# A mixture-of-experts stage on one core: the gated product is turned behind the down products and behind the branch, and the expert counts are read before the first gate and up products

## The chip, the core and the metric

The kernel runs on one core of one Trainium2 chip. A core has five engines that run side by side: TensorE (PE, matrix products; its weight loads are shown as PEld), VectorE (DVE), ScalarE (ACT), GpSimd (POOL) and SyncE (SP, which here only issues transfers). Each engine takes its instructions in order, and waits for the others through semaphores. Products land in PSUM, everything else lies in SBUF, and weights come from HBM by DMA. The metric is the device time of one execution in microseconds.

## The reference, cut to what matters

Two blocks of a model of 256 tokens and width 1024 are computed in float32. The part that is changed is the mixture-of-experts layer of the first block:

```python
def moe_ffn(h, router_w, router_b, w_gate, w_up, w_down):
    t = h.reshape(bsz * seq, d)
    logits = t @ router_w + router_b
    top_v, top_i = lax.top_k(logits, 2)
    gates = jax.nn.softmax(top_v, axis=-1)
    combine = jnp.sum(jax.nn.one_hot(top_i, 8) * gates[..., None], axis=1)
    out = jnp.zeros((bsz * seq, d))
    for e in range(8):
        y_e = (silu(t @ w_gate[e]) * (t @ w_up[e])) @ w_down[e]
        out = out + combine[:, e:e + 1] * y_e
    return out
```

There are 8 experts, each token goes to 2 of them, and an expert's hidden width is 3584. An expert's weights are 3 matrices of 1024 x 3584 in float32, 42 MB (42 x 1,048,576 bytes), and the whole layer reads 336 MB.

## The kernel before

**Stages.** The program runs ten stages one after the other: two mixers, a dense feed-forward stage, the mixture-of-experts stage (`moe`), and then the stages of the second block. Only `moe` is changed. In it the tokens of an expert are gathered into up to 96 slots (`xe`), 32 slots to a group; groups 0 and 1 (64 slots) are called `main`, group 2 is `rest`.

**Blocks.** An expert's hidden width is worked off in 7 blocks of 512, so the loop of `moe` passes 56 blocks, i = 0 to 55, expert by expert, and one more pass at its end. A block has three steps:

- `gate_up(i, gs)`: on PE, products of the gathered tokens with the block's gate and up weights (line 1098), then on ACT the silu of the gate half (line 1102) and on DVE its product with the up half (line 1103). The result is the tile `gs`.
- `turn_g(i, gs)`: on PE, transposes of `gs` (line 1110; two for `main`, one for `rest`), and an ACT copy to the tile `gT` (line 1112).
- `down(i, gs)`: on PE, products of `gT` with the block's down weights into an accumulator of the expert (line 1126).

`down` runs one block late (`LAG = 1`): pass i does `gate_up(i)`, then `down(i - 1)`, then `turn_g(i)`. The steps for `rest` stand in a block `tc.If(counts[e] > 64)` (line 1191), so they run only for experts that got more than 64 tokens. On the chip each engine takes that branch by itself; an engine that skips the body still brings its semaphores to the values that the body would have left. In the first pass of an expert the `rest` part of `down` belongs to the expert before and has an If of its own. Another If (line 1180), in pass 15, skips a large body that handles experts with more than 96 tokens; these inputs do not need it.

**Order.** The instructions are laid out by a scheduler before the kernel runs. It gives each engine one fixed order, picks by the order of the source and by when it thinks that operands will be there, and treats an If as one piece. So the order on PE in the trace is not always that of the source: `turn_g`'s transposes stand in some blocks ahead of `down`'s products and in others behind them, and half of `down` can stand behind the If. `tc.issue_after(ins)` forces what is traced inside it to be issued behind `ins` on the engine of `ins`, without a wait.

**Weights.** The layer's 336 MB come as 336 units of 1 MB, in the order of use: 4 units of gate and up for block i, then 2 of down for block i - 1. SP issues one transfer for each unit (line 217). A unit needs a buffer; in this stage there are 16 of them, 15 later on. At the end of pass i, `W.give` hands back the buffers of the block's 4 units and of the 2 of `down`, and the next 6 units are issued into them when PE has passed the last reader, the If included.

**Counts.** `R.counts` holds the tokens of each expert. `values_load_multi_w_load_instructions` (line 1171) loads it into registers of all engines, for the branches to compare. In the source it stands behind the first `gate_up`.

Of the kernel before, what the change touches and what calls it, by code (L numbers as in the profile page):

```python
# [20 lines left out]
T = 256  # L21
NE = 8
# [250 lines left out]
def model(ctx, tc, A, out, stages=STAGES):  # L273
    nc = tc.nc
# [94 lines left out]
    def bank(tag="mm"):  # L369
        p = mm if tag == "mm" else acc  # L370
        return p.tile([128, 512], F32, tag=tag, name=tag)
# [673 lines left out]
    def moe(R, nout, pool):  # L1045


        nb = F1 // 512
# [13 lines left out]
        def gather(p):  # L1062
            S[p] = pool.tile([128, 2, 2, SLOTS], F32R, tag="S", name="S", bufs=2)
            for t in range(2):
                for e in range(2):
                    nc.vector.tensor_scalar(S[p][:, t, e], iota[:, :SLOTS], R.pos[:, t, 2 * p + e:2 * p + e + 1],
                                            R.sel[:, t, 2 * p + e:2 * p + e + 1], ALU.is_equal, ALU.mult)
            xe[p] = pool.tile([128, 8, 2, SLOTS], F32, tag="xe", name="xe", bufs=2)
            w = 2 * SLOTS
            for j in range(4):  # L1070
                ps = bank()
                for i in range(2):
                    k = 2 * j + i
                    o = ps[:, i * w:(i + 1) * w]
                    for t in range(2):
                        s = S[p][:, t].rearrange("p e s -> p (e s)")
                        nc.tensor.matmul(o, R.h[t][:, k * 128:(k + 1) * 128], s, start=t == 0, stop=False)
                        nc.tensor.matmul(o, R.l[t][:, k * 128:(k + 1) * 128], s, start=False, stop=t == 1)
                v = ps[:, :2 * w].rearrange("p (k e s) -> p k e s", k=2, e=2)
                if j % 2:  # L1080
                    nc.vector.tensor_copy(xe[p][:, 2 * j:2 * j + 2], v)
                else:
                    nc.scalar.activation(xe[p][:, 2 * j:2 * j + 2], v, AF.Copy)

        def strips(gs):

            return [(g, c) for g in gs for c in range(4 // len(gs))]

        def gate_up(i, gs):
            e, b = seq[i]  # L1090
            if ("gu", i) not in held:
                held["gu", i] = [W.hold(((("moe", e), "gu", b), j)) for j in range(4)]
            units = held["gu", i]
            n = 256 * len(gs)
            ps = bank()
            for k in range(8):
                for j, (g, c) in enumerate(strips(gs)):
                    nc.tensor.matmul(ps[32 * j:32 * j + 32, :n], xe[e // 2][:, k, e % 2, 32 * g:32 * g + 32],  # L1098
                                     units[k // 2][0](k % 2, c * n, n), start=k == 0, stop=k == 7)
            s = prod[i, gs] = tp.tile([128, 512], F32, tag="g32", name="gs", bufs=4)[:, :n // 2].rearrange("p (q c) -> p q c", c=128)  # L1100
            v = ps[:, :n].rearrange("p (q s c) -> p q s c", s=2, c=128)
            nc.scalar.activation(s, v[:, :, 0], AF.Silu)  # L1102
            nc.vector.tensor_tensor(s, v[:, :, 1], s, op=ALU.mult)  # L1103

        def turn_g(i, gs):

            s, n = prod.pop((i, gs)), len(gs)
            ps = bank()
            for q in range(n):
                nc.tensor.transpose(ps[:, q * 128:(q + 1) * 128], s[:, q], ident)  # L1110
            a = gT[i, gs] = pool.tile([128, n, 128], F32, tag=f"gT{gs[0]}", name="gT", bufs=LAG + 1)
            nc.scalar.activation(a, ps[:, :n * 128].rearrange("p (q c) -> p q c", q=n), AF.Copy)

        def down(i, gs):
            e, b = seq[i]
            if ("d", i) not in held:
                held["d", i] = [W.hold(((("moe", e), "d", b), j)) for j in range(2)]
            units = held["d", i]
            n, w = len(gs), 256 * len(gs)
            if b == 0:  # L1120
                y[e, gs] = bank("acc")
            a, o = gT.pop((i, gs)), y[e, gs]
            for k in range(4):
                for j, (g, c) in enumerate(strips(gs)):
                    at = (k // n + (g - gs[0]) * 2) * 32
                    nc.tensor.matmul(o[32 * j:32 * j + 32, :w], a[:, k % n, at:at + 32], units[k // 2][0](k % 2, c * w, w),  # L1126
                                     start=b == 0 and k == 0, stop=b == nb - 1 and k == 3)
            if b == nb - 1:
                if e not in yf:
                    yf[e] = pool.tile([SLOTS, D], F32, tag="yf", name="yf", bufs=1)  # L1130
                    nc.gpsimd.memset(yf[e][64:SLOTS], 0.0)
                for j, (g, c) in enumerate(strips(gs)):
                    r, v = yf[e][32 * g:32 * g + 32, c * w:(c + 1) * w], o[32 * j:32 * j + 32, :w]
                    if j % 2:
                        nc.vector.tensor_copy(r, v)
                    else:
                        nc.scalar.activation(r, v, AF.Copy)

        def back(e):
            yh, yl = (a.rearrange("p c t -> p (c t)")[:SLOTS] for a in xt())  # L1140
            nc.scalar.activation(yh, yf[e], AF.Copy)
            nc.vector.tensor_tensor(yl, yf[e], yh.bitcast(F32), op=ALU.subtract)
            ST = pool.tile([SLOTS, 2, 128], F32R, tag="ST", name="ST", bufs=1)
            ps = bank()
            for t in range(2):
                nc.tensor.transpose(ps[:SLOTS, t * 128:(t + 1) * 128], S[e // 2][:, t, e % 2, :].bitcast(F32), ident)
            nc.scalar.activation(ST, ps[:SLOTS, :256].rearrange("p (t s) -> p t s", t=2), AF.Copy)

            def scatter(ts=range(2)):
                for t in ts:  # L1150
                    for q in range(2):
                        ps = bank()
                        for n, a in enumerate((yh, yl)):
                            nc.tensor.matmul(ps, ST[:, t, :], a[:, q * 512:(q + 1) * 512], start=n == 0, stop=n == 1)
                        xs = X[t][:, q * 512:(q + 1) * 512]
                        nc.vector.scalar_tensor_tensor(xs, ps, R.comb[:, t, e:e + 1], xs, ALU.mult, ALU.add)
            todo.append(scatter)


        main, rest = (0, 1), (2,)  # L1160
        n = len(seq)
        gather(0)
        for i in range(n + LAG):
            j = i - LAG
            now, late = [], []
            if i < n:
                e, b = seq[i]
                gate_up(i, main)
                now.append(lambda: gate_up(i, rest))
            if i == 0:  # L1170
                _, counts = nc.values_load_multi_w_load_instructions(R.counts[0:1, :NE + 1], min_val=0, max_val=T,
                                                                     skip_runtime_bounds_check_because="the values are only compared")
            if i == 2:
                R.gates()
            if i == n - 2:
                nout.post = post_of(A["final_g"])
            while todo:
                todo.popleft()()
            if i == 2 * nb + 1:
                with tc.If(counts[NE] > SLOTS):  # L1180
                    for base in range(SLOTS, T, 128):
                        second(R, base)
            if j >= 0:
                down(j, main)
                (now if i < n and seq[j][0] == e else late).append(lambda: down(j, rest))
            if i < n:
                turn_g(i, main)
                now.append(lambda: turn_g(i, rest))
            for at, fs in ((j, late), (i, now)):
                if fs:  # L1190
                    with tc.If(counts[seq[at][0]] > 64):  # L1191
                        for f in fs:
                            f()
            W.give(held.pop(("gu", i), []) + held.pop(("d", j), []))
            if j >= 0 and seq[j][1] == nb - 1:
                back(seq[j][0])
            if i < n and e % 2 == 1 and b == nb - 3 and e < NE - 1:
                gather(e // 2 + 1)
        last = todo.popleft()
# [149 lines left out]
```

## Time and profile before

| what | value |
|---|---|
| three runs | 2337.69, 2341.61, 2342.85 us; median 2341.61 |
| the profiled execution's own time | 2337.93 us |
| its span, first to last instruction | 2336.1 us (1.8 us lie around it) |
| PE busy over the span | 2227.8 us, 95% |
| DVE, ACT, POOL busy | 40%, 34%, 7% |
| mean granted TensorE clock | 0.989 |
| HBM read | 595 MB, 255 GB/s over the span |

The trace is that of one execution. Times in it are microseconds from the first instruction; the `moe` stage's products run from 434.3 to 1298.9. An engine's busy share says little here, since matmuls overlap one another; what counts is the time from the start of one step to the start of the next, and the idle time that a row shows in brackets.

### The profile page before, as it was taken

The numbers are of one execution on the slowest core, as the hardware profiler recorded it, in microseconds if no ns is written. First come the engines' busy times: TensorE is split into PE (matmuls) and PEld (weight loads), VectorE is DVE, ScalarE is ACT, GpSimd is POOL, SyncE is SP. The second block draws the span as 40 slices with busy tenths as digits, with TensorE's granted clock in tenths as the row PEclk, the third lists the DMA queues.
The fourth block names the chain that finished last, engine by engine and source line by source line (L and its number), as shares of the span: only waits on it lengthen the run. The fifth ranks groups of instructions, "written<-read, shape, count | busy, mean of one in ns | idle before, by whom it ended". The sixth has DMA issues, their size and how long they took to land. (4 is left out here: it accounts for less than half of the span.)

```text
span 2336.1 us, 36130 instructions
## 1 busy us (share of the span) xinstructions
PE 2227.8 (95%) x15276; PEld 1487.4 (64%) x15276; DVE 926.2 (40%) x1246; ACT 793.3 (34%) x1243; POOL 172.5 (7%) x258
## 2 busy tenths in 40 slices
PE   8999999899989999999998899989999999989998
PEld 7888888434433333333432588877888888877887
DVE  5655565201010101010010554577544644686544
ACT  5544444201010101011010444466444534575443
POOL 3000013000000000000000200061000100050000
PEclk9999999899999999999999999999999999999999
DMA  7655555799979999999999655441555555423552
GB/s 272 226 186 192 180 202 184 288 419 419 420 296 370 382 419 419 401 397 419 420 420 397 250 182 186 152 163 46 198 186 190 183 180 184 154 108 117 182 186 85
DMA packets 89436, 599.09 MB, mean 256 GB/s; under 512 B 12092, under 2 KB 14558, under 8 KB 18460
## 3 DMA queue, kind: packets, MB, share of 16 engines
q1 hardware_dynamic: 88956, 595.81, 65.8%
q8 instruction: 144, 2.36, 0.4%
q10 hardware_dynamic: 288, 0.52, 0.1%
q14 instruction: 48, 0.39, 0.0%
HBM read 595.25 MB, written 1.05 MB: 255 GB/s over the span
## 5 line engine op out<-in xcount | busy, mean ns | idle before, releaser
L238 DVE TENSOR_TENSOR wl<-raw,wh 128x1024 fp32r<-128x1024 f32 (+2 forms) x456 | 540.3, 1215 | 429.0 <-ACT wh L237 428.6
L237 ACT ACTIVATE wh<-raw 128x1024 fp32r<-128x1024 f32 (+2 forms) x456 | 454.6, 1036 | 482.6 <-PE mm L398 302.2
L1098 PE MATMUL mm<-raw,xe 128*32 128x512 f32 (+1 forms) x5376 | 504.2, 525 | 2.7 <-DVEq L1191 1.8
L395 PE MATMUL mm<-wh,xhl 128*128 128x512 f32 (+3 forms) x1280 | 473.5, 372 | 3.1 <-ACT xhl L414 3.1
L396 PE MATMUL mm<-wl,xhl 128*128 128x512 f32 (+3 forms) x1280 | 471.9, 371 | 0.5 <-DVE wl L238 0.5
L398 PE MATMUL mm<-wh,xhl 128*128 128x512 f32 (+3 forms) x1280 | 394.4, 371 | 0.6 <-DVE xhl L415 0.6
L1098 PEld LDWEIGHTS mm<-raw,xe 128*32 128x32 f32 x5376 | 181.3, 111 | 296.3 <-issue 251.0
L1103 DVE TENSOR_TENSOR gs<-mm,gs 128x256 f32<-128x256 f32 (+1 forms) x84 | 31.9, 380 | 688.4 <-ACT gs L1102 590.9
L395 PEld LDWEIGHTS mm<-wh,xhl 128*128 128x128 f32 x1280 | 241.8, 189 | 43.9 <-ACT xhl L414 3.5
L1126 PE MATMUL acc<-raw,gT 128*32 128x512 f32 (+1 forms) x2688 | 266.0, 526 | 3.5 <-PEq L1191 2.7
L396 PEld LDWEIGHTS mm<-wl,xhl 128*128 128x128 f32 x1280 | 241.7, 189 | 41.3 <-DVE wl L238 1.3
L398 PEld LDWEIGHTS mm<-wh,xhl 128*128 128x128 f32 x1280 | 236.8, 189 | 41.5 <-DVE xhl L415 1.7
L1102 ACT ACTIVATE gs<-mm 128x256 f32<-128x256 f32 (+1 forms) x84 | 29.2, 348 | 593.4 <-PE mm L1098 593.4
L395 PE MATMUL acc<-wh,ghl 128*128 128x512 f32 x464 | 186.3, 401 | 0.0
L396 PE MATMUL acc<-wl,ghl 128*128 128x512 f32 x464 | 183.6, 396 | 0.0
L1126 PEld LDWEIGHTS acc<-raw,gT 128*32 128x32 f32 x2688 | 82.6, 110 | 133.4 <-issue 109.6
L398 PE MATMUL acc<-wh,ghl 128*128 128x512 f32 x464 | 145.4, 394 | 0.0
L378 POOL TENSOR_SCALAR s<-s 128x1 f32<-128x1 f32 (+1 forms) x60 | 32.3, 538 | 1152.4 <-ACT junk L385 1050.8
L398 PEld LDWEIGHTS acc<-wh,ghl 128*128 128x128 f32 x464 | 87.4, 188 | 20.6
L396 PEld LDWEIGHTS acc<-wl,ghl 128*128 128x128 f32 x464 | 87.7, 189 | 18.9
L395 PEld LDWEIGHTS acc<-wh,ghl 128*128 128x128 f32 x464 | 87.5, 189 | 18.6
L1110 PEld LDWEIGHTS mm<-c,gs 128*128 128x128 f32 x140 | 16.6, 140 | 105.3 <-DVE gs L1103 38.4
(254 smaller groups left out, 1642.5 us busy)
## 6 DMA issues: line engine op xcount, KB each, us to landing
raw<-in_w_moe_dram SPq DMA_DIRECT2D x336, 1024.0 KB
raw<-in_w_f_dram SPq DMA_DIRECT2D x132, 1024.0 KB
raw<-in_w_ffn_dram SPq DMA_DIRECT2D x42, 1024.0 KB
raw<-in_w_mix_dram SPq DMA_DIRECT2D x23, 1024.0 KB
raw<-in_w_mla_dram SPq DMA_DIRECT2D x18, 1024.0 KB
raw<-in_w_mla_dram SPq DMA_DIRECT2D x8, 576.0 KB
raw<-in_w_mla_dram SPq DMA_DIRECT2D x4, 768.0 KB
c<-in_cst_dram SPq DMA_DIRECT2D x2, 1024.0 KB
```

The costliest lines, as they stand in the source:

```text
L237: self.nc.scalar.activation(h[:, s], t, AF.Copy)
L238: self.nc.vector.tensor_tensor(l[:, s], t, h[:, s].bitcast(F32), op=ALU.subtract)
L378: nc.gpsimd.tensor_scalar(r, ms, EPS, None, ALU.add)
L395: nc.tensor.matmul(o, sh[:, k, :], h[:, j, a:b], start=first and i == 0, stop=False)
L396: nc.tensor.matmul(o, sh[:, k, :], l[:, j, a:b], start=False, stop=False)
L398: nc.tensor.matmul(o, sl[:, k, :], h[:, i + (r[0] if r else 0), a:b], start=False, stop=last and i == n - 1)
L1098: nc.tensor.matmul(ps[32 * j:32 * j + 32, :n], xe[e // 2][:, k, e % 2, 32 * g:32 * g + 32], units[k // 2][0](k % 2, c * n, n), start=k == ...
L1102: nc.scalar.activation(s, v[:, :, 0], AF.Silu)
L1103: nc.vector.tensor_tensor(s, v[:, :, 1], s, op=ALU.mult)
L1110: nc.tensor.transpose(ps[:, q * 128:(q + 1) * 128], s[:, q], ident)
L1126: nc.tensor.matmul(o[32 * j:32 * j + 32, :w], a[:, k % n, at:at + 32], units[k // 2][0](k % 2, c * w, w), start=b == 0 and k == 0, stop=b ...
```

## The change

The read of the counts moves ahead of the loop, and the first `gate_up`'s instructions on PE are queued behind PE's own load of them. `down` returns its last matmul. `turn_g(i, main)` moves behind the If, and its instructions on PE are queued behind that last matmul of `down(i - 1, main)`. `turn_g(i, rest)` stays in the If.

```diff
             for k in range(4):
                 for j, (g, c) in enumerate(strips(gs)):
                     at = (k // n + (g - gs[0]) * 2) * 32
-                    nc.tensor.matmul(o[32 * j:32 * j + 32, :w], a[:, k % n, at:at + 32], units[k // 2][0](k % 2, c * w, w),
-                                     start=b == 0 and k == 0, stop=b == nb - 1 and k == 3)
+                    last = nc.tensor.matmul(o[32 * j:32 * j + 32, :w], a[:, k % n, at:at + 32], units[k // 2][0](k % 2, c * w, w),
+                                            start=b == 0 and k == 0, stop=b == nb - 1 and k == 3)
...
+            return last.ins
...
         gather(0)
+        loads, counts = nc.values_load_multi_w_load_instructions(R.counts[0:1, :NE + 1], min_val=0, max_val=T,
+                                                             skip_runtime_bounds_check_because="the values are only compared")
         for i in range(n + LAG):
             j = i - LAG
             now, late = [], []
             if i < n:
                 e, b = seq[i]
-                gate_up(i, main)
+                with nullcontext() if i else tc.issue_after(next(x.ins for x in loads if x.ins.engine == mybir.EngineType.PE)):
+                    gate_up(i, main)
                 now.append(lambda: gate_up(i, rest))
-            if i == 0:
-                _, counts = nc.values_load_multi_w_load_instructions(R.counts[0:1, :NE + 1], min_val=0, max_val=T,
-                                                                     skip_runtime_bounds_check_because="the values are only compared")
...
+            behind = nullcontext()
             if j >= 0:
-                down(j, main)
+                behind = tc.issue_after(down(j, main))
                 (now if i < n and seq[j][0] == e else late).append(lambda: down(j, rest))
             if i < n:
-                turn_g(i, main)
                 now.append(lambda: turn_g(i, rest))
             for at, fs in ((j, late), (i, now)):
                 if fs:
                     with tc.If(counts[seq[at][0]] > 64):
                         for f in fs:
                             f()
+            if i < n:
+                with behind:
+                    turn_g(i, main)
             W.give(held.pop(("gu", i), []) + held.pop(("d", j), []))
```

## Rows read from the trace of the kernel before

**Rows 1.** Windows, one for each expert's seven blocks: engines' busy time, PEclk, DMA share, GB/s.

```profile
434.50:516.03 81.53, 75.38 (x654) 24.30 (x650) 3.41 (x8) 5.36 (x14) 0.00 (x0) 0.98 0.84 346
516.03:638.60 122.57, 119.62 (x1379) 49.91 (x1375) 11.45 (x23) 12.51 (x34) 0.94 (x1) 1.00 1.01 419
638.60:774.00 135.40, 122.33 (x1379) 46.77 (x1375) 12.32 (x27) 12.56 (x34) 0.94 (x1) 0.97 0.83 337
774.00:866.49 92.49, 86.13 (x764) 29.79 (x760) 10.16 (x18) 9.71 (x22) 0.95 (x1) 1.00 0.99 407
866.49:990.10 123.61, 116.35 (x1347) 46.42 (x1343) 11.39 (x25) 11.71 (x32) 0.94 (x1) 1.00 1.00 411
990.10:1081.19 91.09, 85.52 (x764) 31.15 (x760) 10.26 (x18) 9.60 (x22) 0.94 (x1) 1.00 0.99 405
1081.19:1200.97 119.78, 115.91 (x1348) 46.49 (x1343) 10.33 (x21) 11.54 (x32) 0.95 (x1) 1.00 1.01 419
1200.97:1298.20 97.23, 86.42 (x750) 27.22 (x742) 9.23 (x16) 9.10 (x21) 0.94 (x1) 1.00 0.96 393
```

**Rows 2.** Waits of PE in the stage: total us, times, longest us.

```profile
PE mm L1110 <- DVE gs L1103: 20.2, 22, 1.0
PE mm L1110 <- DVEq L1191: 16.2, 17, 1.0
```

**Rows 3.** Timeline of PE, blocks 16 and 17: start, us, what, idle before.

```profile
694.94 0.44 PE L1110 MATMUL mm<-c,gs 128*128 128x128 f32 x2 [0.96 <-DVE gs L1103]
...
712.36 0.44 PE L1110 MATMUL mm<-c,gs 128*128 128x128 f32 x2 [0.96 <-DVE gs L1103]
```

**Rows 4.** Timeline of PE, block 10 and the start of block 11.

```profile
568.46 7.08 PE L1098 MATMUL mm<-raw,xe 128*32 128x512 f32 x64
...
584.85 0.64 PE L1098 MATMUL mm<-raw,xe 128*32 128x512 f32 x4
```

**Rows 5.** Timeline of PE, block 23 and the start of block 24.

```profile
802.59 7.08 PE L1098 MATMUL mm<-raw,xe 128*32 128x512 f32 x64
810.62 0.44 PE L1110 MATMUL mm<-c,gs 128*128 128x128 f32 x2 [0.95 <-DVEq L1191]
...
814.81 0.64 PE L1098 MATMUL mm<-raw,xe 128*32 128x512 f32 x4
```

**Rows 6.** Timeline of PE, block 2 and the start of block 3.

```profile
457.53 7.07 PE L1098 MATMUL mm<-raw,xe 128*32 128x512 f32 x64
464.42 3.62 PE L1126 MATMUL acc<-raw,gT 128*32 128x512 f32 x32
467.96 0.78 PE L1110 MATMUL mm<-c,gs 128*128 128x128 f32 x2
468.67 0.64 PE L1098 MATMUL mm<-raw,xe 128*32 128x512 f32 x4
```

**Rows 7.** Timeline of all engines, end of block 0.

```profile
442.31 0.33 PE L1110 MATMUL mm<-c,gs 128*128 128x128 f32 x1 [0.96 <-DVE gs L1103]
...
444.57 2.24 SPq L217 DMA_DIRECT2D raw<-in_w_moe_dram  x3
444.60 0.45 PE L1110 MATMUL mm<-c,gs 128*128 128x128 f32 x1 [1.97 <-PEq L1191]
444.98 0.20 PEld L1098 LDWEIGHTS mm<-raw,xe 128*32 128x32 f32 x8 [0.22 <-issue]
```

**Rows 8.** Window between the first and the second block, columns as in rows 1.

```profile
434.50:445.00 10.50, 7.57 (x70) 2.17 (x62) 0.86 (x2) 0.38 (x1) 0.00 (x0) 0.97 0.00 0
```

**Rows 9.** Lines 1171 and 1098 by themselves: ns min/median/max, first and last start in us.

```profile
L1171 PEldq TENSOR_LOAD <-counts x1: 1032/1032/1032, 442.9 to 442.9; - x1
L1098 PEldq EVENT_SEMAPHORE  x86: 51/51/51, 430.3 to 1280.5; - x86
```

**Rows 10.** The branches of lines 1191 and 1180 on PE, same columns.

```profile
L1191 PEldq COMPARE_BRANCH  x96: 65/176/852, 444.1 to 1296.2; - x96
L1180 PEldq COMPARE_BRANCH  x1: 5135/5135/5135, 669.9 to 669.9; - x1
```

## The prediction

> **What bounds the kernel now.** I first cut the mixture-of-experts stage into windows, one for each expert [rows 1]. The number of PE instructions tells which experts run their `rest` part: experts 1, 2, 4 and 6 with some 1350 products ("heavy"), 0, 3, 5 and 7 with some 760 ("light"). The reader should look at the last two columns. Where the loads run without a break they move 419 GB/s at a share of 1.01, so a unit of 1.0486 MB takes 2.50 us and the 6 units of a block 15.0. PE takes less than that for a light block and more for a heavy one [rows 3 to 6]. So two things set the time by turns: PE's chain, block after block, and behind it the loads, with 16 buffers between them that let either run ahead by 40 us at most.
>
> How near the loads are follows from a ledger of units in stock when an expert begins. It is 16 at 434.5 (the loads stand still, all buffers are full [rows 8]); an expert adds its GB/s times its window divided by 1.0486 and takes 42 (the first 40, for `down` lags). From rows 1: 16 + 26.9 - 40 = 2.9 units when expert 1 begins, then 9.9, 11.4, 5.3, 11.8, 5.0 and 10.9 when experts 2 to 7 begin. It never reaches nothing, so today PE sets the stage, but three times it is within a few units of it. And in expert 2 the share is 0.83: buffers are full there and the loads wait for PE.
>
> Then I asked what PE waits for. The largest groups are waits of the transposes (line 1110) for the silu and product of the block just computed: 39 waits, 36.4 us [rows 2]; where the releaser is "DVEq L1191" it is the same wait, ended beside DVE's branch. One is block 0's [rows 7], four stand before the `rest` transposes in the first blocks of heavy experts (7, 14, 28, 42). The timeline, block by block, gives the other 34 to the `main` transposes, where these stand ahead of `down` on PE [rows 3, 5]: 17 in heavy blocks, 17 in light ones. By expert, 0 to 7: 2, 2, 6, 5, 6, 3, 3, 7. In the other blocks the transposes already stand behind `down`, and there is no such wait [rows 4, 6].
>
> **The wait that goes.** Behind the change the `main` transposes cannot be issued before `down`'s last product. The silu and product of DVE and ACT then run behind `down`'s 3.5 us (464.42 to 467.96) [rows 6] in place of 0.95 us of idle PE. The price I take is the whole step from block to block, since a wait also empties PE's pipeline. Heavy: 712.36 - 694.94 = 17.42 with the wait [rows 3], 584.85 - 568.46 = 16.39 without [rows 4], so 1.03. Light: 814.81 - 802.59 = 12.22 [rows 5] against 468.67 - 457.53 = 11.14 [rows 6], so 1.08. The sum is 17 x 1.03 + 17 x 1.08 = 35.9 us.
>
> What is late next? `gT` is made at the end of pass i and read by `down(i)`, a whole `gate_up` (6.9 us [rows 6]) later: nothing is late. `rest`'s transposes and its four waits stay where they are. In light blocks PE still has to let its last product retire before it brings its semaphore up to date behind the skipped body. Today the second transpose pays for that: 0.71 us from the first transpose to the next block [rows 6], in which the two take 0.78 us instead of the 0.44 that they take with no branch between them [rows 3]. I expect the 0.34 to be paid as before, by `down`'s end, and take nothing for it; the bounds are a gain and a loss of 0.34 in each of 28 light blocks, 9.5 us either way.
>
> **The move behind the branch.** The transposes are 2 products and 1 ACT copy in each of 56 blocks, no transfer. The next `gate_up` already stands behind the branch, so nothing new queues there. In the light blocks with the wait, today's branch comes ahead of `down`, and the 4 units of gate and up are freed some 2 us earlier in the block than they will be. While loads are behind, several transfers are queued on SP, so I take this at nothing; with no queue it would delay a load by 2 us, once for each stretch in which the loads are behind (three, 6 us).
>
> **The counts.** Today block 0 ends with a wait of 0.96, then PE's own load of the counts (1.03 us [rows 9]) and the branch, between the two transposes; the second comes at 444.60 and block 1 at 444.98 [rows 7]. The loads stand still over all of it, from 434.5 to 445, and are let go at 444.57 by the branch [rows 7, 8]. With the counts already there PE passes the branch when `gate_up(0)` is through, near 441.4 (442.31 less 0.96), so the loads restart 3.1 us earlier. Block 0 has no `down`, so its wait of 0.96 stays; the second transpose then follows at once, and block 1 starts near 442.75: 2.2 us. Block 1 took 12.55 us (444.98 to 457.53), 1.41 more than block 2 [rows 6, 7]; the window's granted clock is 0.98, so part of it ran at 1.2 GHz, against 1.00 (2.4 GHz) in the later light experts [rows 1]. Waits of 0.96 leave 1.00 in expert 4; the 3.6 us here, from 441.4 to 445, come before the fall, so I take the 1.4 as gained (bounds 0 and 1.4). The load itself: PE's sequencer waits on a semaphore for the first `gate_up` at 430.3 [rows 9], while that block's first weights go in after 434.3, so some 4 us of gather products are queued ahead and cover a load of 1.03. Without that cover it costs that much, or up to 2.0, the whole wait that stands between the two transposes today [rows 7].
>
> **The sum on PE.** 35.9 + 2.2 + 1.4 = 39.5 us. By expert: 5.8, 2.1, 6.2, 5.4, 6.2, 3.2, 3.1, 7.6.
>
> **What the loads give back.** The same ledger with shorter windows. Expert 0: 3.1 of the 5.8 us come with earlier loads, so 2.7 / 2.5 = 1.1 units fewer, 1.8 in stock. Expert 1: 120.5 us bring 48.2, stock 8.0. Expert 2: 129.2 us could bring 51.7, but the stock cannot pass today's 11.4; the loads idle for 6.3 units. Expert 3: 33.7 (its 87.1 us less today's small break), 3.1. Expert 4: 47.0, 8.1. Expert 5: 35.2, 1.3. Expert 6: 46.7, 6.0. Expert 7: 35.8 against 44, so 2.2 units, 5.5 us, too late. Where an expert begins with 1.8 or 1.3 units, the fourth unit of its first block lands after (4 - 1.8) x 2.5 = 5.5 or 6.8 us and is wanted after 5.2, three quarters of a `gate_up`: 0.3 and 1.6 us of waiting, of which the 1.6 comes off the 5.5 later. In all about 6 us. 39.5 - 6 = 33.5, and for the coarse ledger I take 33. The loads, no longer PE, then set the end of the stage.
>
> Against its own time the sum gives 2337.9 - 33 = 2304.9. The median of the runs is 3.7 above that execution, so I count from midway, 2340: **2307 us**. A measurement of this kernel tells 0.2%, 4.7 us, from no change.
>
> **Rivals.** *Loads always find room* (0.10): if the scheduler's order frees buffers earlier than my ledger has it, all 39.5 come through: 2300. For: 6.3 units are idle in expert 2 only because buffers are full. Against: ledger ends of 1.8 and 1.3 units.
>
> *Half the wait stays* (0.14): in light blocks the retiring before the skip costs 0.34 more, or `down`'s halves land so that PE still waits: gain 18 to 24, 2319. For: half of `down` stands behind the If in heavy blocks today.
>
> *The loads bind already* (0.05): only the 3.1 us of the earlier restart come through, 2337. For: share 1.01 in experts 1 and 6. Against: 0.83 in expert 2 and stocks of 10 units and more [rows 1]. The Trainium skill, DMA: Bandwidth & Descriptors, Specifications, gives a core 358 GB/s from HBM; by that a unit would take 2.93 us (an estimate from that page), the 320 units after the restart 938 us, more than the stage lasts, and nothing could be gained. The trace does not agree: it moves 419 [rows 1].
>
> *The transposes fall behind the next `gate_up`* (0.07): the edge keeps them behind `down(i - 1)`, but nothing keeps them ahead of `gate_up(i + 1)`. Then `down(i)` stands right behind them and PE waits for a transpose, ACT's copy and two semaphores, about 0.95 as the mirrored wait does [rows 3], in all 55 blocks: 52 us for the 35.9 saved, less 3.6 at the opening, 2353. It decides once more than some 40 blocks go that way. Against: `gs` is ready 1 us after `gate_up`, long before.
>
> *A skip costs a fetch* (0.02): the branch over the large body held PE for 5.1 us [rows 10]. If the 28 skips in light blocks did, less the 3.5 us of `down` queued ahead, 45 us would come on top: 2352. Against: no branch of line 1191 took more than 0.85, half of them under 0.18 [rows 10], and the bodies stay the same. The Trainium skill, Runtime: NRT & Kernel Launch, Instruction fetch mechanics, says that a taken branch to instructions outside a small window has to fetch them first, which speaks against hanging more behind a branch; the trace shows it at line 1180 and not at line 1191.
>
> **Chances.** The forecast has 0.62, the rivals 0.10, 0.14, 0.05, 0.07 and 0.02. Faster by over 0.2%: 0.62 + 0.10 + 0.14 = 0.86; same 0.05; slower 0.09. The forecast's own range is 2300 to 2314 (coarse ledger, clock, the 2 us of later freeing). The range asked for runs from the first rival with 4 of the 9.5 us that retiring may give, 2296, to the second with the 6 us of later freeing on top, 2326 in round numbers.
>
> **What the new profile would show.** No idle time of about 0.95 before line 1110 in `main`; blocks of 16.4 and 11 us; loads restarting near 442; PE waiting for loads of the units around blocks 42 and 55, with shares near 1.01 from expert 3 on. Waits of line 1126 for line 1112 would show the fourth rival, and a share under 0.9 in the last expert would show the ledger wrong.

## The result and the profile after

The changed kernel takes 2320.1 us (median of four runs, 2318.1 to 2322.0) against 2342.2 for the kernel before (four runs): a ratio of 0.9905, 95% interval 0.9883 to 0.9927, so 22 us faster. The forecast was 2307 with a range of 2296 to 2326: the direction and the range hold, the gain is two thirds of the 33 us forecast. In the profiled executions the stage, from the first product of line 1098 to the last of `down`, takes 843.3 us (437.32 to 1280.60) where it took 865.9 (434.27 to 1300.21 in the kernel before): 22.7 us, about the difference of the medians. As wholes the two profiled executions differ by 16.9 us (2337.9 and 2321.0), since the unchanged stages around `moe` took 5.8 us longer in the one after; so the stage is what is compared below.

The products, the transposes and `down` keep their lines (1098, 1110, 1126); the two Ifs stand at 1181 and 1192 now.

The windows by expert, with the columns of [rows 1]:

```profile
437.32:516.89 79.57, 77.26 (x655) 22.81 (x654) 3.53 (x8) 5.28 (x14) 0.00 (x0) 1.00 0.90 371
516.89:640.09 123.20, 122.30 (x1376) 49.84 (x1375) 11.23 (x23) 12.52 (x34) 0.94 (x1) 1.00 1.01 416
640.09:765.61 125.52, 120.04 (x1377) 46.77 (x1376) 12.25 (x27) 12.40 (x34) 0.94 (x1) 0.99 0.88 356
765.61:853.58 87.97, 86.22 (x762) 28.95 (x761) 10.17 (x18) 9.49 (x22) 0.94 (x1) 1.00 1.00 411
853.58:970.39 116.81, 115.60 (x1344) 45.09 (x1343) 11.32 (x25) 11.48 (x32) 0.94 (x1) 1.00 1.01 419
970.39:1063.42 93.03, 87.43 (x761) 29.47 (x761) 10.35 (x18) 9.55 (x23) 0.95 (x1) 1.00 1.01 419
1063.42:1184.80 121.38, 118.73 (x1344) 45.63 (x1344) 10.19 (x21) 11.36 (x32) 0.94 (x1) 1.00 1.01 420
1184.80:1280.60 95.80, 88.52 (x763) 25.94 (x762) 9.23 (x16) 9.16 (x22) 0.94 (x1) 1.00 0.99 405
```

Read beside [rows 1]: expert 2 is 10 us shorter, experts 3 and 4 together 11; but experts 5 and 6, forecast to gain 3 us each, are each some 2 us longer than before. There the mean share is 1.01: the loads hardly stand still.

The waits of PE in the stage, as in [rows 2]:

```profile
PE mm L1098 <- DMA raw<-in_w_moe_dram: 5.1, 10, 0.7
PE acc L1126 <- DMA raw<-in_w_moe_dram: 4.1, 8, 0.7
PE acc L1126 <- PEq L1192: 4.0, 19, 0.4
PE mm L1110 <- DVE gs L1103: 2.9, 4, 0.7
PE mm L1110 <- DVEq L1192: 1.7, 2, 1.0
```

The 36.4 us in front of the transposes have become 4.6: block 0's, which stays, `rest`'s four, and one of 0.76 before the `main` transposes of block 36, which is new. In their place stand waits for loads, 18 of them (9.2 us), which the kernel before did not have.

The timeline of PE in a heavy block (17), a light one (23) and in block 2, to be held against [rows 3, 5, 6]:

```profile
700.07 7.07 PE L1098 MATMUL mm<-raw,xe 128*32 128x512 f32 x64
...
716.08 0.44 PE L1110 MATMUL mm<-c,gs 128*128 128x128 f32 x2
716.45 1.07 PE L1098 MATMUL mm<-raw,xe 128*32 128x512 f32 x8
...
793.26 7.07 PE L1098 MATMUL mm<-raw,xe 128*32 128x512 f32 x64
...
802.23 1.92 PE L1126 MATMUL acc<-raw,gT 128*32 128x512 f32 x16 [0.18 <-PEq L1192]
...
804.45 1.06 PE L1098 MATMUL mm<-raw,xe 128*32 128x512 f32 x8
...
458.18 7.07 PE L1098 MATMUL mm<-raw,xe 128*32 128x512 f32 x64
465.07 1.02 PE L1126 MATMUL acc<-raw,gT 128*32 128x512 f32 x2
466.25 3.63 PE L1126 MATMUL acc<-raw,gT 128*32 128x512 f32 x30
...
470.18 0.64 PE L1098 MATMUL mm<-raw,xe 128*32 128x512 f32 x4
```

The heavy block takes 16.38 and the light one 11.19, as forecast. Block 2, which had no wait before, has become longer: 12.00 in place of 11.14. A product of `down` is two instructions in the trace; of its 16 products one (x2) now stands ahead of the If and 15 (x30) behind it. The timeline shows such a split (1 and 15, in two blocks 5 and 11), or a block longer by as much, in 14 blocks: 1 to 4, 9 to 12, 26, 37, 40, 44 to 46. Where the split is 8 and 8, as in blocks 17 and 23, next to nothing is lost.

Last, the blocks before and after the change of expert from 5 to 6:

```profile
1058.46 1.92 PE L1126 MATMUL acc<-raw,gT 128*32 128x512 f32 x16 [0.65 <-DMA raw<-in_w_moe_dram]
1060.86 1.92 PE L1126 MATMUL acc<-raw,gT 128*32 128x512 f32 x16 [0.47 <-DMA raw<-in_w_moe_dram]
1062.71 0.44 PE L1110 MATMUL mm<-c,gs 128*128 128x128 f32 x2
1063.42 1.92 PE L1098 MATMUL mm<-raw,xe 128*32 128x512 f32 x16 [0.28 <-DMA raw<-in_w_moe_dram]
1065.82 1.92 PE L1098 MATMUL mm<-raw,xe 128*32 128x512 f32 x16 [0.47 <-DMA raw<-in_w_moe_dram]
```

PE takes a unit every 2.4 to 2.6 us here, each as it lands: this is the loads' pace, not PE's. The same is seen in blocks 54 and 55.

So two suspects for the missing 11 us: the split of `down` (14 blocks by some 0.83, 11.6 us on PE), or the loads. The experiments set them against each other.

### The profile page after: what moved, and what is told of

It is laid out like the page before. It is cut to its first block, busy times and chain, and to the rows that moved or that the text cites. A ratio compares the mean times of both kernels' runs of the same rounds, so it can differ in the third digit from the quotient of the medians.

```text
span 2319.3 us, 36153 instructions
## 1 busy us (share of the span) xinstructions
PE 2238.7 (97%) x15276; PEld 1482.4 (64%) x15276; DVE 926.1 (40%) x1246; ACT 792.6 (34%) x1243; POOL 172.7 (7%) x258
## 5 line engine op out<-in xcount | busy, mean ns | idle before, releaser
L1098 PEld LDWEIGHTS mm<-raw,xe 128*32 128x32 f32 x5376 | 168.9, 110 | 301.5 <-issue 245.2
L1126 PE MATMUL acc<-raw,gT 128*32 128x512 f32 (+1 forms) x2688 | 280.6, 523 | 12.4 <-DMA raw<-in_w_moe_dram 4.1
L398 PEld LDWEIGHTS mm<-wh,xhl 128*128 128x128 f32 x1280 | 236.9, 189 | 41.5 <-DVE xhl L415 1.5
L1126 PEld LDWEIGHTS acc<-raw,gT 128*32 128x32 f32 x2688 | 90.0, 109 | 168.2 <-issue 128.3
L1112 ACT ACTIVATE gT<-mm 128x256 f32<-128x256 f32 (+1 forms) x84 | 29.1, 347 | 202.7 <-PE mm L1110 201.4
```

The lines of the kernel that those rows point to most:

```text
L398: nc.tensor.matmul(o, sl[:, k, :], h[:, i + (r[0] if r else 0), a:b], start=False, stop=last and i == n - 1)
L1126: last = nc.tensor.matmul(o[32 * j:32 * j + 32, :w], a[:, k % n, at:at + 32], units[k // 2][0](k % 2, c * w, w), start=b == 0 and k == 0, ...
```

## Experiments

Each ratio is to the kernel before, run on the same chip in turn; 95% intervals in brackets.

| kernel | median, us | ratio to before |
|---|---|---|
| the change | 2320.1 | 0.9905 [0.9883, 0.9927] |
| counts_only | 2335.3 | 0.9980 [0.9969, 0.9990] |
| turn_only | 2321.1 | 0.9915 [0.9902, 0.9928] |
| turn_ahead_of_if | 2322.8 | 0.9931 [0.9916, 0.9946] |
| one_strip_twice | 2323.2 | 0.9934 [0.9917, 0.9951] |
| turn_ahead_half_down | 2299.4 | 0.9826 [0.9808, 0.9845] |
| before_half_down | 2303.6 | 0.9851 [0.9835, 0.9867] |
| after_14_buffers | 2334.2 | 0.9976 [0.9967, 0.9985] |
| give_early | 2318.6 | 0.9910 [0.9895, 0.9925] |
| before_17_buffers | 2337.0 | 0.9970 [0.9960, 0.9980] |
| after_17_buffers | 2319.7 | 0.9900 [0.9887, 0.9913] |
| turn_ahead_17_buffers | 2318.0 | 0.9892 [0.9879, 0.9905] |
| give_early_17_buffers | 2317.2 | 0.9885 [0.9871, 0.9899] |

The kernel before had a median of 2339.6 beside the first four experiments, 2340.3 beside the next four and 2344.3 beside the last four, so the ratios are the numbers to compare.

### The split of down: turn_ahead_of_if

```diff
+            if i < n:
+                with behind:
+                    turn_g(i, main)
             for at, fs in ((j, late), (i, now)):
                 if fs:
                     with tc.If(counts[seq[at][0]] > 64):
                         for f in fs:
                             f()
-            if i < n:
-                with behind:
-                    turn_g(i, main)
```

> The transposes stay queued behind down's last product, but are traced ahead of the If again; in this order all 16 of down's products stand ahead of the If, in one piece, in every block inside an expert. Theory (the 11 us that the change fell short of its forecast are 14 blocks in which the If was put behind the first or the fifth of down's products, 0.85 us each): blocks of 11.1 and 16.4 everywhere, 12 us less on PE, of which the later 5 are given back to waits for loads at blocks 41 to 42 and 54 to 55: 2313 us (2309 to 2317). Rival (loads set the time of the changed kernel, whatever PE does): 2320, no change against the changed kernel. Second rival (going behind the branch is what brings the gain): most of it is lost, 2330 and more.

The time did not fall: the first theory is wrong, the first rival right. It is not that the edit failed on PE. Blocks 3 and 12 of this kernel, on PE's timeline:

```profile
467.55 7.07 PE L1098 MATMUL mm<-raw,xe 128*32 128x512 f32 x64
474.44 3.62 PE L1126 MATMUL acc<-raw,gT 128*32 128x512 f32 x32
...
604.47 7.07 PE L1098 MATMUL mm<-raw,xe 128*32 128x512 f32 x64
611.36 3.62 PE L1126 MATMUL acc<-raw,gT 128*32 128x512 f32 x32
...
620.86 1.49 PE L1098 MATMUL mm<-raw,xe 128*32 128x512 f32 x12
```

`down` is in one piece (x32), the heavy block takes 16.39 in place of the changed kernel's 17.21. Expert 0, which the edit shortens most, takes 76.1 us in place of 79.6. Then PE runs into the loads in the first block of expert 1 (timeline of PE):

```profile
512.52 3.98 PE L1098 MATMUL mm<-raw,xe 128*32 128x512 f32 x32
517.33 1.92 PE L1098 MATMUL mm<-raw,xe 128*32 128x512 f32 x16 [0.83 <-DMA raw<-in_w_moe_dram]
...
523.63 1.92 PE L1126 MATMUL acc<-raw,gT 128*32 128x512 f32 x16 [1.88 <-DMA raw<-in_w_moe_dram]
526.03 1.93 PE L1126 MATMUL acc<-raw,gT 128*32 128x512 f32 x16 [0.48 <-DMA raw<-in_w_moe_dram]
```

and its waits for loads over the stage, by the view of waits, are twice those of the changed kernel, 18.4 us in place of 9.2:

```profile
PE mm L1098 <- DMA raw<-in_w_moe_dram: 9.2, 16, 1.0
PE acc L1126 <- DMA raw<-in_w_moe_dram: 9.2, 13, 1.9
```

What PE saves by the whole `down` is handed over to the loads. The stage is even 3.7 us longer than that of the change; 2.3 of these lie in block 15, at the large If, and not at a load. The second rival falls as well: going behind the branch is not what brings the gain.

### What a lone product costs: one_strip_twice

```diff
+            steps = [(k, j, g, c) for k in range(4) for j, (g, c) in enumerate(strips(gs))]
+            if n == 2:
+                steps.insert(1, steps.pop(4))
-            for k in range(4):
-                for j, (g, c) in enumerate(strips(gs)):
+            for k, j, g, c in steps:
```

> As turn_ahead_of_if, but in every down of main the fifth product is moved to the second place, so that the first two use the same strip of 32 columns of the array one after the other; no branch stands between them. Theory (four products on four strips run side by side, and one that has no partners takes the place of four): 5 places of about 0.87 us in each down in place of 4, 55 x 0.85 = 47 us on PE, less up to 10 us that go into today's waits for loads: 2351 to 2361. Rival (what the changed kernel lost is the drain at the branch between the first product and the rest, not the lone product): under 0.2 us for each block, 2313 to 2325.

The rival's number came, but not by its reason only. Block 1 on PE's timeline, up to the start of block 2:

```profile
443.14 7.07 PE L1098 MATMUL mm<-raw,xe 128*32 128x512 f32 x64
454.31 1.07 PE L1098 MATMUL mm<-raw,xe 128*32 128x512 f32 x8
```

Such blocks take 11.17 in place of 11.15, so two products in a row on one strip cost 0.02: products behind them on other strips are not held up. What costs 0.83 in the changed kernel is therefore not the order of the products. That leaves the border between the two parts. The reading that fits is that the array has to be empty there: with one product on one side and 15 on the other, the fullest strip then has 1 + 4 products in place of 4. It fits all three forms seen: 1 and 15 as well as 5 and 11 (2 + 3) cost one place more, 8 and 8 (2 + 2) none. In light blocks the border is the skipped If; in heavy ones it is argued, not shown, that it is `rest`'s transpose, which takes all strips. The Trainium skill, TensorEngine Tiling (Array Packing), Key Properties, says that a change of tiling mode drains the engine and that different tiles can run in parallel. The 0.02 agrees with the second; the first could hold in the heavy blocks, but no run shows it, and at the If of a light block no mode changes.

### The loads: half of down's bytes

```diff
+            key = self.plan[self.loaded][0]
+            if key[0][0][0] == "moe" and key[0][1] == "d":
+                c //= 2
...
-units[k // 2][0](k % 2, c * w, w)
+units[k // 2][0](0, c * w, w)
```

> As turn_ahead_of_if, but each unit of down's weights is loaded only by its first half, and the products of its second half read the first half again (so the result is that of other weights): PE does the same products, the loads have 5 units' bytes for a block in place of 6. Theory (in turn_ahead_of_if the loads set the time at blocks 7, 28, 42 and 55, and what PE saves turns into waits for them): the waits of some 24 us in blocks 7, 27, 28, 40 to 42, 54 and 55 go, 2322.8 - 24 = 2299 us (2294 to 2304). Rival (PE's own order sets it, and the loads only seem to be waited for): 2318 to 2323.

> The kernel before with the same halved loads of down's weights. The scheduler, which plans with the loads, now lays out all of down ahead of the transposes by itself in every block inside an expert. Theory: the time of turn_ahead_half_down plus the 2.9 us of the later counts, 2302 us (2297 to 2307); so without the loads' pressure the edit of the transposes is worth nothing, and the 0.95 us waits come from where the scheduler expects down's second unit to be late. Rival (with fewer loads the kernel before keeps its time, since its loads are hidden): 2337 to 2341.

Both came out as the theory has it: 2299.4 for 2299 and 2303.6 for 2302. In turn_ahead_half_down PE issues the same products as in turn_ahead_of_if; with a sixth of the bytes gone the waits for loads in the stage shrink from 18.4 to 1.8 us, and the kernel is 23 us faster. The scheduler lays out a few blocks otherwise, but that cancels: the blocks that waited for loads (7, 27, 28, 39 to 42, 54 and 55) make up 22.4 of the 22.5 us by which the stage is shorter. The view of waits of turn_ahead_half_down:

```profile
PE mm L1101 <- DMA raw<-in_w_moe_dram: 1.8, 1, 1.8
```

The stage takes 824.4 us: 41.5 less than before the change, about the gain that PE alone would have brought. before_half_down is the kernel before with nothing changed but the bytes, and in its order all of `down` stands ahead of the transposes in every block inside an expert. One of its heavy blocks on PE's timeline:

```profile
710.72 7.07 PE L1101 MATMUL mm<-raw,xe 128*32 128x512 f32 x64
717.61 3.62 PE L1129 MATMUL acc<-raw,gT 128*32 128x512 f32 x32
721.16 0.33 PE L1113 MATMUL mm<-c,gs 128*128 128x128 f32 x1
...
727.11 7.07 PE L1101 MATMUL mm<-raw,xe 128*32 128x512 f32 x64
```

So the 34 waits of [rows 2] come from an order that the scheduler chose because of the loads: with fewer bytes to load it does not choose it. That it believed `down`'s units to be late is inferred from this. On the chip they were there (the kernel before has no wait for a load), and PE waited for `gs` instead. The edit corrects that.

### Buffers and their return

after_14_buffers leaves out the entry `[(lent(tp, "ghl"), end)] * 2`; the kernels with 17 add one, and move `yf` into a tile that stands idle:

```diff
+                 + [(lent(tp, "ghl"), end)] * 2 + [(lent(pool, "more"), end)])
...
+                    yf[e] = tp.tile([128, D], F32, tag="junk", name="yf", bufs=1)[:SLOTS]
```

> The changed kernel with 14 buffers for units in place of 16 (the two that another tile lends are left out). Theory (the loads set the changed kernel's end, and what they can gain is how little they stand still for full buffers): two units less in stock when expert 2 ends, 2 x 2.5 = 5 us later, 2325 (2322 to 2329). Rival (PE sets it): no slower, and up to 4 us faster, since in this order the If splits down in fewer blocks: 2316 to 2320.

The sign is that of the loads' theory: 14 us lost though fewer blocks split `down`. The size is three times what I expected. 5 us of it I had left out (argued, not measured): two units fewer are in stock when the loads stand still before the stage, so 322 in place of 320 have to come behind. And PE's waits for loads doubled (10.2 and 9.5 us in the view of waits). 1.7 us of the profiled execution have nothing to do with buffers: its block 0 takes 10.60 in place of 8.87, at a granted clock of 0.80 over its products.

> The kernel before with a 17th buffer for units in this stage (room is made by putting yf into a tile that stands idle). Theory (in the kernel before PE sets the time and the loads have a little room to spare): worth no more than the two waits that the scheduler's new order no longer has, 2340 less 2, 2336 to 2341. Rival (the kernel before is already set by the loads): 5 to 7 us faster, 2333 to 2335.

> The changed kernel with the same 17th buffer. Theory (the loads set the changed kernel's end): 14 buffers cost 14 us, so one more brings half of that, 7 us: 2313 (2310 to 2316). Rival (PE's order sets it): 2319 to 2321.

> turn_ahead_of_if with the same 17th buffer. Its PE has some 12 us less to do than the changed kernel's, since down is never split. Theory (loads set both): 7 us faster than with 16, 2816 less 500, that is 2316 us (2312 to 2319), no better than after_17_buffers. Rival (PE sets the time once the loads have room): 12 us below after_17_buffers, near 2302.

("2816 less 500" is a slip; 2323 less 7 is meant.) Measured by ratio, the extra buffer brings the kernel before 7 us, the changed kernel nothing (0.9900 for 0.9905), and turn_ahead_of_if 0.4%, some 9 us. None of the three follows the theory in size. The first lies in the theory's range as a time (2337.0), but the kernel before took 2344.3 beside it, so by ratio it is the rival's 7. A reason for the second is seen in part: block 0 alone is 1.8 us longer, as the granted clock shows, columns as in [rows 1], `gate_up(0)` of the changed kernel first, then with 17 buffers:

```profile
437.32:444.39 7.07, 7.07 (x65) 1.98 (x64) 0.56 (x1) 0.28 (x1) 0.00 (x0) 1.00 0.01 3
```

```profile
435.99:444.86 8.87, 8.87 (x65) 2.18 (x64) 0.56 (x1) 0.18 (x1) 0.00 (x0) 0.79 0.20 84
```

and block 29 is 2.4 us longer, 1.86 of them a wait of line 1155's products for the copy of line 1142, which the scheduler put into this block here. In the kernel before, another buffer made the scheduler lay out blocks 13, 15, 23 and 24 otherwise, which are 6.9 us shorter together, and block 29, which is 5.4 longer; PE waits for loads there for 0.2 us in all, so the rival's reason is not seen. These three runs change too much at once to weigh a buffer; what they do show is that a PE with nearly 12 us less to do (turn_ahead_17_buffers) is not 12 us below after_17_buffers, but 2: the rival falls.

```diff
+            W.give(held.pop(("gu", i), []))
             if i < n:
                 with behind:
                     turn_g(i, main)
-            W.give(held.pop(("gu", i), []) + held.pop(("d", j), []))
+            W.give(held.pop(("d", j), []))
```

> The changed kernel, but the 4 units of gate and up are handed back in the source right behind the If, and only down's 2 at the end of the pass. Theory (loads set the end): in heavy blocks the buffers come free up to 2.2 us earlier, half of down and the transposes, once for the stretch in which buffers are full: 1 to 3 us faster, 2317 to 2319. Rival (PE sets it): 2320, no change.

> The changed kernel with both: the 17th buffer, and gate's and up's units handed back right behind the If. Theory: the gains add, since both take from the time in which the loads stand still: after_17_buffers less 1.5, 2311.5 (2308 to 2315). Rival (with more buffers the early return brings nothing): as after_17_buffers.

1.5 us faster by the medians, but 0.9910 against 0.9905 by ratio: not told apart from nothing. With both, 0.9885 is the best ratio measured, and its interval overlaps that of the change; no version is shown to beat it.

### The counts

counts_only is the kernel before with the read of the counts moved as in the change; turn_only is the change with the read left where it was.

> The kernel before with the counts read ahead of the first gate_up and nothing else. Theory: the opening alone, 1.8 us from block 0 to block 1 and 0.6 in block 1, 2.4 us, hence 2339.8 against 2342.2. Rival (PE's own load of the counts is not hidden in front of gate_up): no change or up to 1 us slower. Rival (loads set the end, so their restart 3 us earlier counts whole): 3.1 us faster.

> The changed kernel with the read of the counts back behind the first gate_up. Theory: the changed kernel's 2320.1 plus the 2.4 us of the opening, 2322.5. Rival (loads set the end of the stage from the opening on): plus 3 us or more, 2323 and more. If the opening were worth nothing: 2320.

Alone the counts bring 0.2%, 4.4 us by the medians [2.3 to 7.3]; the stage of the profiled execution is 2.9 us shorter. That they bring nothing is ruled out, but the theory's 2.4 and the last rival's 3.1 both lie in the interval. The opening of counts_only, timeline of all engines, answers to [rows 7]:

```profile
441.99 0.33 PE L1110 MATMUL mm<-c,gs 128*128 128x128 f32 x1 [0.96 <-DVE gs L1103]
442.50 2.63 SPq L217 DMA_DIRECT2D raw<-in_w_moe_dram  x4
442.53 0.30 PE L1110 MATMUL mm<-c,gs 128*128 128x128 f32 x1 [0.21 <-PEq L1191]
442.76 3.21 PE L1098 MATMUL mm<-raw,xe 128*32 128x512 f32 x28
```

The 1.97 us between the transposes are 0.21, and block 1 starts 8.80 us after block 0 (10.71 before) and takes 11.15 (12.55 before). On top of the moved transposes the same move brings nothing that can be told, 0.9905 against 0.9915. PE's timeline of turn_only shows why:

```profile
443.87 0.44 PE L1110 MATMUL mm<-c,gs 128*128 128x128 f32 x2 [0.96 <-DVEq L1192]
444.71 1.50 PE L1098 MATMUL mm<-raw,xe 128*32 128x512 f32 x12 [0.40 <-ACTq L1192]
```

With both transposes behind the If, PE's load of the counts fits into the 0.96 us in which PE waits for `gs` anyhow; block 0 takes 8.88 us with the counts late and 8.87 with the counts early.

## Why the prediction was right, and where its size was off

**The wait that goes: right.** The plain ones of the 34 blocks went from 17.42 to 16.38 and from 12.22 to 11.19, forecast 16.39 and 11.14; their waits of [rows 2] are gone. By the timelines the 34 blocks are 26.7 us shorter, and 35.9, the forecast's own figure, without the 9.2 of waits for loads that now stand in five of them. Retiring ahead of a skip cost 0.18 behind `down`'s first half, inside the bounds.

**That other blocks stay as they were: wrong, and it cost next to nothing.** The forecast gave no price to the place of the If among `down`'s products. The new edge let the scheduler put the If behind the first product, 14 times some 0.83 us on PE. But the kernel without those splits is no faster, so they mostly fill time in which PE would have waited for loads. Block 15 was not priced either: it is 3.4 us shorter (29.5 to 26.1), the wait behind the large If in it 2.9 in place of 4.1. So the 22.7 us are 26.7 in the 34 blocks, 2.4 in the opening (blocks 0 and 1, with block 1's split), 3.4 in block 15 and 0.9 elsewhere, less 10.7 in the 13 other split blocks.

**The opening: right in size, wrong in what brings it.** 3.6 us were forecast, from the counts; counts_only measures 2.9 in its stage and 4.4 by the medians. In the change, moving the transposes behind the branch would have brought most of it alone. The count load is hidden, as forecast.

**What the loads give back: the step that failed.** The forecast had 6 of 39.5 us given back. For turn_ahead_of_if, where PE's saving is whole, it was 41.5 - 19.0 = 22.5 (its stage takes 847.0 us, with halved bytes 824.4). For the change 39.5 - 22.7 = 17 are missing, mainly 9.2 of waits for loads and 11.6 of splits, less block 15's 3.4. That the loads would bind, and at blocks 42 and 55, was right; the stock was too high. The ledger, replayed with the windows after: 16 + 28.2 - 40 = 4.2 units when expert 1 begins, then 11.0, 11.6, 4.1, 8.8 and, at 1063.42, 4.0. But at 1063.42 PE waits for the very unit that it takes next, and for each one after it. So of the 4.0 in this ledger one unit is there, the one that has just landed; 3.0 are not. 1.2 are not weights at all but fetched instructions, 1.10 + 0.14 MB up to that moment by the view of the DMA queues:

```profile
q1 hardware_dynamic: 34081, 248.24, 96.1%
q8 instruction: 67, 1.10, 0.7%
q14 instruction: 17, 0.14, 0.1%
```

The other 1.8 are bytes of later units, moved while this one was not complete: several transfers are under way at once, and a ledger of bytes counts them all. The Trainium skill, DMA: Bandwidth & Descriptors, Two DMAs through the same engine are not ordered, says that nothing orders transfers across the 16 engines, and that data has landed once the full semaphore count is there; the 1.8 units of this trace are in line with it.

The last unit is also wanted 1.9 us (0.8 units) before the stage's end, which the forecast's ledger left out. With both, its last step would have read 2.2 + 3.0 + 0.8 = 6.0 units too late, 15 us, and the gain 39.5 - 15 = 24.5. That is a sum made after the result, and it does not settle the size: the 22.7 measured hold the splits and block 15, and turn_ahead_of_if gave back 22.5, 7.5 more than these 15, for which I have no account. Nor are 3.0 units off everywhere. In turn_ahead_of_if the ledger reads 2.0 when expert 1 begins, and PE does find two units; only the third, at 517.33, comes 1 unit (2.4 us) later than the ledger has it, while at expert 6 it reads 4.0 and PE waits for the second. So the ledger's error grows along the stage. A second omission was smaller: the wait was counted up to the fourth unit of an expert's first block, while `down`'s two, wanted only 1.7 us later, wait longer, 1.88 in block 7.

**Rivals.** "The loads bind already" was nearer the truth than its 0.05: not in the kernel before, which got 4.4 us from the counts and had no wait for a load, but once PE is quicker. "Half the wait stays" has the measured time almost to the microsecond (2319) and is wrong all the same: no half of the wait stayed. The transposes did not fall behind the next `gate_up`. Skips of the small If cost next to nothing, but one branch on PE did take much longer than the 0.85 of [rows 10]:

```profile
L1192 PEldq COMPARE_BRANCH  x96: 65/176/3642, 441.7 to 1276.6; - x96
```

The 3.64 us fall in block 37, where the products queued ahead cover all but some 0.2 (12.21 in place of 11.99). What held the branch is not shown.

Not settled: why two buffers fewer cost 14 us and one more brings the change nothing, and how much of the 22.7 us comes from fewer stops of the loads in expert 2 (share 0.83 before, 0.88 after) and how much from the stock that the kernel before still had at its end.

## What to carry to other kernels

When two chains take turns in setting the time, a saving on one is worth only the slack of the other, so measure that slack where the other chain hands over, by the first wait that it would cause, and not by bytes moved. Cut the bytes of one stream in an experiment before you polish the other: that one run showed what all of PE's saving could be worth (41.5 us) and what was left of it (19 to 23). And when a planner orders the work, ask what it believed to be late: the waits removed here came from a load that was in time.

## What the runs showed of the hardware

Two products in a row on the same strip of 32 columns do not hold up products for other strips behind them (0.02 us in a block), while a skipped branch set one product after the start of a group of 16 costs 0.83 us, and in the middle of the group 0.05. And the granted clock over the 64 instructions of block 0 was 1.00 in the change and 0.79 with a 17th buffer (a mean over 2.4 and 1.2 GHz), with the same order of instructions on PE in that block: 7.07 and 8.87 us. It did not fall there. In both kernels it was 0.50 over the gather products just ahead (425.00 to 437.20 and 425.00 to 435.90); in the change it rose right before block 0, with the 17th buffer 3.7 us into it, as the window of these 3.7 us shows:

```profile
435.99:439.70 3.71, 3.71 (x21) 0.98 (x24) 0.56 (x1) 0.18 (x1) 0.00 (x0) 0.51 0.47 197
```

So this was a level left over from before block 0. Why it rose later in the one is open.
